# The first feed-forward product as 2x2 blocks, seven block products for eight, in three of four quarters

## The chip, the core and the metric

The kernel runs on one core of a Trainium2 chip. Measured is the device time of one call in microseconds. TensorE (PE) multiplies a stationary 128x128 weight with moving columns; VectorE (DVE), ScalarE (ACT) and GpSimd (POOL) do the elementwise work; SyncE (SP) issues the DMAs from DRAM. PEld is the weight load of TensorE.

## The reference

One step of a two-layer backbone over 640 tokens (128 of context, 512 latents) with 1024 features. A layer has a mixing part (three groups of heads and an output projection) and a feed-forward part of width 4096. The change concerns the second:

```python
h = rmsnorm(x, p['norm2_g']) * (1.0 + scale2) + shift2
x = x + gate2 * (relu(h @ W1) ** 2 @ W2)      # W1: 1024 x 4096, W2: 4096 x 1024
```

Shift, scale and gate (the modulation) come from a condition through a linear layer of each layer's own, with one column for the context's tokens and one for the latents'.

## The kernel before

Features lie on partitions, tokens along the free axis: x is eight tiles of 128 x 640. A product in float32 is made of three TensorE passes on float32r parts: high part of the weights by high part of the input, high by low, low by high. So each weight of 128 x 128 brings 3 x 2 matmuls of 320 columns, since a PSUM bank takes half of the tokens.

`feed_forward` (L1759) goes through the 4096 hidden features in four quarters. A quarter first makes eight units of the first product (f1): a unit is one block of 128 outputs, 8 blocks of input features x 3 passes x 2 halves = 48 matmuls (`fm`, L312 to 318). The input is not the normed one but x times its scale (zh, zl), with the two shifts as two extra columns, so the first half is 322 columns wide; `Norm.out` multiplies the product by 1/rms (un, L552), ACT adds the shift and takes the relu, DVE squares it (u, L1777) and `evac_split` (L306, L307) takes it apart into uh (a cast, ACT) and ul (a subtraction, DVE). Then come eight units of the second product (f2), again 48 matmuls each, that are added to x with the gate by three DVE instructions (`residual`, L565). A unit's PSUM tile (PA) is one of two, so unit m + 2 begins when DVE has emptied that of unit m.

Weights come through `Weights` (L282): a unit is two halves of 128 x 512 (256 KB), each fetched into wr by SP, cast to wh by ACT (L296) and subtracted to wl by DVE (L297).

The modulation of layer 1 is computed beside the feed-forward part of layer 0, as "fill" (`ada_rows`, L452 on): 112 pieces of weight of 256 KB (wa), each multiplied by one condition on POOL (junk, L481, summed by ACT, L482) and by the other on DVE (junk, L484). A fill step is two pieces: two POOL and two DVE products. There are 57 steps; f1 of the first quarter takes one per unit, f1 of the others one per two units, f2 one per unit, and what is left comes behind the last unit.

A scheduler orders the instructions when the program is built, each engine's list is fixed from then on, and an engine works through its list in order. Queues of interest: DVE's (weight splits, residuals, fill), POOL's (fill, the norm's sums of squares, the norm's power r, L257) and SP's (weights, fill, x).

In the last quarter `scaled` and `square` prepare the next layer's norm (zh, zl, L520; nsq, L512). The first product of layer 1 needs r for its first un.

## Time and profile before

| | |
|---|---|
| time, median of 3 runs | 1908.3 us (1906.05 to 1914.73) |
| span of the profiled execution | 1908.2 us |
| instructions | 31581 |
| PE busy | 1778.2 us (93%), 11796 matmuls |
| DVE busy | 1268.1 us (66%) |
| ACT busy | 863.5 us (45%) |
| POOL busy | 599.4 us (31%) |
| mean granted TensorE clock | 0.944 of full speed |

The span runs from the first to the last instruction of one execution. A share of busy time is an average over stages: the feed-forward part of layer 0 ends at 1005.4 us, that of layer 1 with the program.

### The profile page before, as it was taken

Reading aid. Unit: us, or ns where it says so; the run is one execution under the profiler, and the core shown is the slowest. Engines: PE = TensorE matmul, PEld = TensorE weight load, DVE = VectorE, ACT = ScalarE, POOL = GpSimd, SP = SyncE. Lnnn points to the kernel's source line nnn. Section 1 sums busy time; section 2 is a strip of 40 time slices with the busy share of each in tenths; the row PEclk is TensorE's granted clock in tenths of the full one; section 3 lists DMA queues with packets and bytes.
Section 4 is the critical chain, followed back from the end, with each engine's and each line's share of the span. In section 5 each row is a group of like instructions: output and inputs, shape, how many; then the busy total and the mean of one; then the engine's idle time right before and its main releaser. Section 6 shows DMA issues by size and latency. Waiting matters only on the chain. (4 is left out here: it accounts for less than half of the span.)

```text
span 1908.2 us, 31581 instructions
## 1 busy us (share of the span) xinstructions
PE 1778.2 (93%) x11796; PEld 1677.8 (88%) x11796; DVE 1268.1 (66%) x2427; ACT 863.5 (45%) x1921; POOL 599.4 (31%) x650
## 2 busy tenths in 40 slices
PE   6899975989999999999997899889998999999999
PEld 4798864889898998999996888768998999999999
DVE  7785778877879567584688766778657435344352
ACT  5553355765555253452555443376544324132230
POOL 4353345442546124150276455354203000000000
PEclk8998986999899999999997999889999999999999
...
GB/s 295 44 84 38 50 61 87 72 124 136 86 130 162 123 116 145 99 144 117 106 180 92 72 67 32 45 49 71 100 30 62 73 77 73 78 73 73 77 79 82
DMA packets 102329, 176.75 MB, mean 93 GB/s; under 512 B 11808, under 2 KB 27040, under 8 KB 102176
## 3 DMA queue, kind: packets, MB, share of 16 engines
...
q10 hardware_dynamic: 560, 0.18, 0.0%
...
## 5 line engine op out<-in xcount | busy, mean ns | idle before, releaser
L296 ACT CAST wh<-wr 128x512 fp32r<-128x512 f32 (+2 forms) x364 | 225.9, 622 | 560.7 <-PE fm L318 461.4
L297 DVE TENSOR_TENSOR wl<-wr,wh 128x512 fp32r<-128x512 f32 (+1 forms) x340 | 270.8, 802 | 116.7 <-issue 69.4
L481 POOL TENSOR_TENSOR junk<-wa,crow 128x512 f32<-128x512 f32 x112 | 175.2, 1583 | 288.4 <-DVE u L1777 194.5
L318 PE MATMUL fm<-zh,wh 128*128 128x322 f32 (+1 forms) x1088 | 252.2, 315 | 13.8 <-ACT zh L519 8.2
L318 PE MATMUL fm<-zl,wh 128*128 128x322 f32 (+1 forms) x1088 | 253.5, 314 | 2.2 <-DVE zl L520 1.4
L318 PE MATMUL fm<-zh,wl 128*128 128x322 f32 (+1 forms) x1088 | 252.2, 313 | 0.0
L318 PE MATMUL fm<-uh,wh 128*128 128x320 f32 x1024 | 235.8, 312 | 13.1 <-DVE x L565 13.1
L318 PE MATMUL fm<-ul,wh 128*128 128x320 f32 x1024 | 237.2, 311 | 0.1
L318 PE MATMUL fm<-uh,wl 128*128 128x320 f32 x1024 | 234.9, 311 | 0.0
L318 PEld LDWEIGHTS fm<-zh,wh 128*128 128x128 f32 x1088 | 185.6, 192 | 15.1 <-ACT zh L519 8.4
L318 PEld LDWEIGHTS fm<-zl,wh 128*128 128x128 f32 x1088 | 185.9, 192 | 4.0 <-DVE zl L520 2.1
L318 PEld LDWEIGHTS fm<-zh,wl 128*128 128x128 f32 x1088 | 185.9, 192 | 0.2 <-issue 0.2
L318 PEld LDWEIGHTS fm<-uh,wh 128*128 128x128 f32 x1024 | 173.1, 190 | 14.1 <-issue 14.0
L318 PEld LDWEIGHTS fm<-ul,wh 128*128 128x128 f32 x1024 | 173.6, 190 | 0.8 <-DVE ul L307 0.8
L318 PEld LDWEIGHTS fm<-uh,wl 128*128 128x128 f32 x1024 | 173.0, 190 | 0.0
L565 DVE SCALAR_TENSOR_TENSOR x<-fm,mod,x 128x128 f32<-128x128 f32 (+2 forms) x192 | 72.5, 432 | 134.4 <-PE fm L318 134.4
L552 DVE TENSOR_TENSOR un<-fm,nR 128x640 f32<-128x640 f32 x68 | 55.8, 823 | 108.7 <-PE fm L318 108.7
L784 PE MATMUL tm<-wl,hhi 128*128 128x256 f32 (+2 forms) x400 | 120.5, 302 | 4.9 <-POOL wl L297 4.9
L783 PE MATMUL tm<-wh,hhi 128*128 128x256 f32 (+2 forms) x400 | 120.5, 302 | 0.3 <-ACT xpad L628 0.2
L785 PE MATMUL tm<-wh,hlo 128*128 128x256 f32 (+2 forms) x400 | 120.0, 300 | 0.0
L484 DVE SCALAR_TENSOR_TENSOR junk<-wa,crow 128x512 f32<-128x512 f32 x112 | 115.2, 1067 | 0.0
L784 PEld LDWEIGHTS tm<-wl,hhi 128*128 128x128 f32 x400 | 81.2, 203 | 5.8 <-POOL wl L297 5.2
...
## 6 DMA issues: line engine op xcount, KB each, us to landing
...
wa<-in_w_adaT SPq DMA_DIRECT2D x112, 256.0 KB, 3.2
...
xsave<-x SPq DMA_DIRECT2D x24, 320.0 KB, 2.2
x<-xsave SPq DMA_DIRECT2D x24, 320.0 KB, 4.2
x<-in_xT SPq DMA_DIRECT2D x16, 320.0 KB, 5.6
out_yT<-x SPq DMA_DIRECT2D x8, 320.0 KB, 2.2
```

What stands on the lines that cost most here:

```text
L296: act.copy(out=hi[:, :w], in_=raw[:, :w])
L297: (pool if n in ON_POOL else vec).tensor_tensor(out=lo[:, :w], in0=raw[:, :w], in1=f(hi[:, :w]), op=ALU.subtract)
L318: pe.matmul(o, w, xx[k][:, ts], start=s, stop=e)
L481: pool.tensor_tensor(out=junk, in0=raws[i], in1=row[v][h], op=ALU.mult)
L484: vec.scalar_tensor_tensor(out=junk, in0=raws[i], scalar=1.0, in1=row[v][h], op0=ALU.mult, op1=ALU.mult, accum_out=sum_)
L552: vec.tensor_tensor(out=v2(t_), in0=fl[:, 2:1022].rearrange("p (h t) -> p h t", h=2)[:, :, :HT], in1=v2(self.R), op=ALU.mult)
L565: vec.scalar_tensor_tensor(out=x[m][:, t0:t0 + n], in0=src, scalar=mods[l][:, j, m, v:v + 1], in1=x[m][:, t0:t0 + n], op0=ALU.mult, op1=AL ...
L783: pe.matmul(ps[:, i, :n], hh[k][:, ts], hi[:, c:c + n], start=s, stop=False)
L784: pe.matmul(ps[:, i, :n], hh[k][:, ts], lo[:, c:c + n], start=False, stop=False)
L785: pe.matmul(ps[:, i, :n], hl[k][:, ts], hi[:, c:c + n], start=False, stop=e)
```

## The change

The first product of quarters 1 to 3 is made in pairs of units (m and m + 4). The block matrix of two output blocks by two halves of the input features, times two halves of features by two halves of tokens, takes eight block products; the Winograd form of Strassen's scheme takes seven (L1911 on, `pair`): four with sums of weight blocks (S1 to S4, made by POOL, L1791) or sums of input blocks (T1 to T4), and three with plain blocks. A block product is 4 k x 3 passes = 12 matmuls of 320 columns, a pair 84. Three PSUM banks (ffx, ffz, ffy) hold the sums; ACT copies a bank to SBUF between blocks, DVE adds the next bank to it (L1937, L1943, L1945). The square of the relu becomes one DVE instruction (u, L1893), and uh and ul follow as before.

The first quarter stays as it was. During units 0 to 3 of its second product `expanded` makes the normed input, which no longer has extra columns, and the sums T1 to T4 in 28 tiles that live to the end of the layer: per k four pieces on DVE, four on ACT, four POOL subtractions of 128 x 320 (L1869), and the two parts of each. To make room for them x goes to DRAM (xsave) after each unit of every second product and comes back one unit ahead in the next quarter.

Weights come through `Stream` (in place of `Weights` for this part): up to seven halves fetched and two split ahead. A pair's seven weight blocks are split as before (ACT L1804, DVE L1805). Buffers: 48 long tiles for 44, 13 of passage (Y) for 10, 7 raw weights for 4, 5 low parts for 4; the rotary tables moved into long tiles. With 7 raw buffers three more halves are fetched at the program's start. The fill is paced anew: one step per unit in the first quarter's f1, none in pairs, none in units 0 to 3 of the first quarter's f2, two in every other unit of f2.

```diff
-NG, NX, NXS = 44, 6, 10
-NWR, NWH, NWL = 4, 6, 4
+NG, NX, NXS = 48, 6, 13
+NWR, NWH, NWL = 7, 6, 5
...
+    FETCHED, AHEADS = 7, 2
...
+        def pair(self, n1, n2):                       # class Stream
...
+                for key, x0, x1, op in (("S1", "21", "22", ALU.add), ("S2", "S1", "11", ALU.subtract),
+                                        ("S3", "11", "21", ALU.subtract), ("S4", "12", "S2", ALU.subtract)):
+                    box[key] = Y([P, 512], name="wS")
+                    pool.tensor_tensor(out=box[key], in0=box[x0], in1=box[x1], op=op)
...
+            self.src += [(1, lambda key=key: take(key)) for key in ("11", "12", "S2", "S1", "S3", "S4", "22")]
...
+        for k in range(4):                            # expanded
+            h1, h2 = normed(k), normed(k + 4)
...
+            for o, i0, i1 in ((h_(ta, 0), h_(h1, 1), h_(h1, 0)), (h_(ta, 1), h_(h2, 1), h_(ta, 0)),
+                              (h_(tb, 0), h_(h2, 1), h_(h1, 1)), (h_(tb, 1), h_(h2, 0), h_(ta, 1))):
+                pool.tensor_tensor(out=o, in0=i0, in1=i1, op=ALU.subtract)
...
+            go(px, "B11", True)                       # pair
+            act.copy(out=v1[:, 0], in_=px)
+            go(pz, "B21", True)
+            vec.tensor_tensor(out=v1[:, 0], in0=v1[:, 0], in1=pz, op=ALU.add)
+            go(px, "T2", False)
+            act.copy(out=v1[:, 1], in_=px)
+            go(py, "T1", True)
+            act.copy(out=sy, in_=py)
+            go(px, "T3", False)
+            vec.tensor_tensor(out=v2_[:, 1], in0=sy, in1=px, op=ALU.add)
+            go(py, "B22", False)
+            vec.tensor_tensor(out=v1[:, 1], in0=v1[:, 1], in1=py, op=ALU.add)
+            go(px, "T4", False)
+            act.copy(out=v2_[:, 0], in_=px)
...
+                if q and m + 1 < KD:
+                    load_x(xsave, m + 1)
+                if q == 0 and m < 4:
+                    next(expand)
...
+                nc.sync.dma_start(a["yT"][:, m] if l == DEPTH - 1 and q == 3 else xsave[:, m], x[m])
...
+                for _ in range(0 if q == 0 and m < 4 else 2):
                     fill.step()
```

How the lists change, at three places. First, VectorE at the start of the second product of layer 0's second quarter, from behind the residual of unit 0 to that of unit 1 (x is the residual, junk the fill, wl a weight split). Before:

```order
L297 TENSOR_TENSOR wl_8051<-wr_8048,wh_8050 128x512
L297 TENSOR_TENSOR wl_8081<-wr_8078,wh_8080 128x512
L484 SCALAR_TENSOR_TENSOR junk_8283,adares_8272<-wa_8201,crow_6011 128x512
L484 SCALAR_TENSOR_TENSOR junk_8351,adares_8272<-wa_8278,crow_6008 128x512
L491 TENSOR_TENSOR adapt_8203<-adares_7316 128x16
L484 SCALAR_TENSOR_TENSOR junk_8361,adares_8272<-wa_8285,crow_6011 128x512
L565 SCALAR_TENSOR_TENSOR x_5061<-fm_7969,mod_86,x_5061 128x128
L565 SCALAR_TENSOR_TENSOR x_5061<-fm_7969,mod_86,x_5061 128x192
L565 SCALAR_TENSOR_TENSOR x_5061<-fm_7969,mod_86,x_5061 128x320
```
After:

```order
L1805 TENSOR_TENSOR wl_8211<-wr_8113,wh_8210 128x512
L484 SCALAR_TENSOR_TENSOR junk_8171,adares_8051<-wa_8159,crow_6026 128x512
L484 SCALAR_TENSOR_TENSOR junk_8242,adares_8051<-wa_8166,crow_6023 128x512
L484 SCALAR_TENSOR_TENSOR junk_8252,adares_8051<-wa_8173,crow_6026 128x512
L484 SCALAR_TENSOR_TENSOR junk_8256,adares_8051<-wa_8247,crow_6023 128x512
L1805 TENSOR_TENSOR wl_8276<-wr_8178,wh_8275 128x512
L484 SCALAR_TENSOR_TENSOR junk_8266,adares_8051<-wa_8254,crow_6026 128x512
L484 SCALAR_TENSOR_TENSOR junk_8337,adares_8051<-wa_8261,crow_6023 128x512
L565 SCALAR_TENSOR_TENSOR x_7984<-fm_8082,mod_86,x_7984 128x128
L565 SCALAR_TENSOR_TENSOR x_7984<-fm_8082,mod_86,x_7984 128x192
L565 SCALAR_TENSOR_TENSOR x_7984<-fm_8082,mod_86,x_7984 128x320
```
Six fill products stand between the two residuals, where three stood; seven stand ahead of the first of them, and the next units have seven and five. GpSimd's list at that place, before (fill alone, spread over f1 and f2):

```order
L481 TENSOR_TENSOR junk_8191<-wa_8116,crow_6010 128x512
L481 TENSOR_TENSOR junk_8196<-wa_8123,crow_6009 128x512
L481 TENSOR_TENSOR junk_8275<-wa_8194,crow_6010 128x512
L481 TENSOR_TENSOR junk_8280<-wa_8201,crow_6009 128x512
L481 TENSOR_TENSOR junk_8353<-wa_8278,crow_6010 128x512
```
After, the last weight sums of the pairs (wS) and the start of the fill:

```order
L1791 TENSOR_TENSOR wS_7704<-wr_7698,wr_7700 128x512
L1791 TENSOR_TENSOR wS_7706<-wS_7704,wr_7696 128x512
L1791 TENSOR_TENSOR wS_7708<-wr_7696,wr_7698 128x512
L1791 TENSOR_TENSOR wS_7710<-wr_7702,wS_7706 128x512
L481 TENSOR_TENSOR junk_8054<-wa_7371,crow_6025 128x512
L481 TENSOR_TENSOR junk_8059<-wa_7378,crow_6024 128x512
L481 TENSOR_TENSOR junk_8068<-wa_8057,crow_6025 128x512
L481 TENSOR_TENSOR junk_8073<-wa_8064,crow_6024 128x512
```
The fill that follows is 26 products in a row; the next weight sums stand behind them.

Second, VectorE in the first product of layer 1. Before, one unit:

```order
L552 TENSOR_TENSOR un_18812<-fm_18751,nR_16175 128x640
L297 TENSOR_TENSOR wl_18903<-wr_18900,wh_18902 128x512
L1777 TENSOR_TENSOR u_3937_18819<-relu_18816 128x640
L297 TENSOR_TENSOR wl_18933<-wr_18930,wh_18932 128x512
L307 TENSOR_TENSOR ul_18822<-u_3937_18819,uh_18821 128x640
```
After, the larger part of one pair (v is what ACT copied out of PSUM, ffx, ffy and ffz are the banks):

```order
L1937 TENSOR_TENSOR v_3884_17590<-v_3884_17590,ffz_17588 128x320
L1805 TENSOR_TENSOR wl_17678<-wr_17450,wh_17677 128x512
L1805 TENSOR_TENSOR wl_17695<-wr_17593,wh_17694 128x512
L1805 TENSOR_TENSOR wl_17712<-wr_17599,wh_17711 128x512
L1943 TENSOR_TENSOR v_3885_17591<-sy_17592,ffx_17587 128x320
L1805 TENSOR_TENSOR wl_17763<-wS_17603,wh_17762 128x512
L1945 TENSOR_TENSOR v_3884_17590<-v_3884_17590,ffy_17589 128x320
L1805 TENSOR_TENSOR wl_17780<-wS_17601,wh_17779 128x512
L1893 SCALAR_TENSOR_TENSOR u_3909_17728<-v_3884_17590 128x640
L1805 TENSOR_TENSOR wl_17797<-wS_17605,wh_17796 128x512
L1893 SCALAR_TENSOR_TENSOR u_3912_17734<-v_3885_17591 128x640
L307 TENSOR_TENSOR ul_17731<-u_3909_17728,uh_17730 128x640
```
A pair (two units) has seven splits, three additions from PSUM and four instructions of 640, where two units had four splits and six of 640; no fill stands here in either.

Third, VectorE behind the last unit of layer 0, to the norm's v, on which r and the first un of layer 1 rest. Before:

```order
L520 SCALAR_TENSOR_TENSOR zl_11145<-x_5379,amul_89,zh_11144 128x512
L720 TENSOR_REDUCE ls_11607<-lp_11606 128x2
L484 SCALAR_TENSOR_TENSOR junk_11169,adares_10890<-wa_11160,crow_6008 128x512
L484 SCALAR_TENSOR_TENSOR junk_11179,adares_10890<-wa_11167,crow_6011 128x512
L484 SCALAR_TENSOR_TENSOR junk_11183,adares_10890<-wa_11174,crow_6008 128x512
L722 TENSOR_TENSOR nlam_11609<-le_11608 128x1
L484 SCALAR_TENSOR_TENSOR junk_11193,adares_10890<-wa_11181,crow_6011 128x512
L723 TENSOR_SCALAR nlam_11609<-nlam_11609 128x1
L484 SCALAR_TENSOR_TENSOR junk_11197,adares_10890<-wa_11188,crow_6008 128x512
L484 SCALAR_TENSOR_TENSOR junk_11207,adares_10890<-wa_11195,crow_6011 128x512
L484 SCALAR_TENSOR_TENSOR junk_11211,adares_10890<-wa_11202,crow_6008 128x512
L535 TENSOR_SCALAR v_2427_11310<-nss_11304 128x5
```
After:

```order
L520 SCALAR_TENSOR_TENSOR zl_11462<-x_11328,amul_89,zh_11461 128x128
L520 SCALAR_TENSOR_TENSOR zl_11462<-x_11328,amul_89,zh_11461 128x512
L720 TENSOR_REDUCE ls_11855<-lp_11854 128x2
L722 TENSOR_TENSOR nlam_11857<-le_11856 128x1
L723 TENSOR_SCALAR nlam_11857<-nlam_11857 128x1
L535 TENSOR_SCALAR v_2580_11558<-nss_11552 128x5
```
The nine products between zl and v are gone from there; all fill stands ahead of the last residual.

## Rows read from the trace of the kernel before

**Rows 1.** Page, busy time of the engines; DMA rate in the 40 slices.
```profile
PE 1778.2 (93%) x11796; PEld 1677.8 (88%) x11796; DVE 1268.1 (66%) x2427; ACT 863.5 (45%) x1921; POOL 599.4 (31%) x650
...
GB/s 295 44 84 38 50 61 87 72 124 136 86 130 162 123 116 145 99 144 117 106 180 92 72 67 32 45 49 71 100 30 62 73 77 73 78 73 73 77 79 82
```

**Rows 2.** Busy us per engine, TensorE clock, DMA share, GB/s: quarters, then the layers' border.
```profile
652.10:771.80 119.70, 115.40 (x770) 114.92 (x770) 79.53 (x131) 49.76 (x114) 36.84 (x24) 0.99 0.40 124
...
1005.40:1035.40 30.00, 17.19 (x112) 16.63 (x110) 24.06 (x41) 14.92 (x37) 24.71 (x19) 0.78 0.34 104
1449.70:1563.20 113.50, 112.98 (x770) 112.72 (x769) 51.01 (x83) 34.79 (x66) 2.79 (x2) 1.00 0.26 75
1563.20:1676.70 113.50, 113.50 (x770) 113.50 (x769) 49.40 (x80) 34.25 (x65) 0.00 (x0) 1.00 0.26 75
```

**Rows 3.** VectorE in time, a first-product unit of layer 1: start, us, operation.
```profile
1584.63 0.82 DVE L552 TENSOR_TENSOR un<-fm,nR 128x640 f32<-128x640 f32 x1 [1.77 <-PE fm L318]
1585.37 0.68 DVE L297 TENSOR_TENSOR wl<-wr,wh 128x512 fp32r<-128x512 f32 x1
...
1589.21 0.83 DVE L307 TENSOR_TENSOR ul<-u,uh 128x640 fp32r<-128x640 f32 x1 [0.29 <-ACT uh L306]
1591.79 0.82 DVE L552 TENSOR_TENSOR un<-fm,nR 128x640 f32<-128x640 f32 x1 [1.75 <-PE fm L318]
```

**Rows 4.** VectorE, residuals of two neighbouring second-product units, layer 1.
```profile
1641.55 1.14 DVE L565 SCALAR_TENSOR_TENSOR x<-fm,mod,x 128x128 f32<-128x128 f32 x3 [2.77 <-PE fm L318]
...
1648.58 1.13 DVE L565 SCALAR_TENSOR_TENSOR x<-fm,mod,x 128x128 f32<-128x128 f32 x3 [2.77 <-PE fm L318]
```

**Rows 5.** TensorE in time, output projection of layer 1, single matmuls.
```profile
1400.22 0.31 PE L318 MATMUL wo<-mixh,wl 128*128 128x320 f32 x1
1400.37 0.30 PE L318 MATMUL wo<-mixh,wh 128*128 128x320 f32 x1
```

**Rows 6.** VectorE in time, second quarter of layer 0, first alone, then beside POOL.
```profile
712.62 0.69 DVE L484 SCALAR_TENSOR_TENSOR junk<-wa,crow 128x512 f32<-128x512 f32 x1
...
713.23 1.81 DVE L484 SCALAR_TENSOR_TENSOR junk<-wa,crow 128x512 f32<-128x512 f32 x1
...
714.97 1.77 DVE L297 TENSOR_TENSOR wl<-wr,wh 128x512 fp32r<-128x512 f32 x1
716.67 1.92 DVE L307 TENSOR_TENSOR ul<-u,uh 128x640 fp32r<-128x640 f32 x1
...
726.49 1.13 DVE L565 SCALAR_TENSOR_TENSOR x<-fm,mod,x 128x128 f32<-128x128 f32 x3
```

**Rows 7.** GpSimd in time, the same stretch.
```profile
700.61 1.30 POOL L481 TENSOR_TENSOR junk<-wa,crow 128x512 f32<-128x512 f32 x1 [1.36 <-DVE ul L307]
...
720.99 8.40 POOL L481 TENSOR_TENSOR junk<-wa,crow 128x512 f32<-128x512 f32 x5 [0.64 <-DVE junk L484]
```

**Rows 8.** Waits of TensorE: us in total, times, longest.
```profile
PE fm L318 <- DVE x L565: 15.8, 5, 4.5
...
PE nrb L544 <- POOL r L257: 9.2, 2, 8.8
...
PE fm L318 <- ACT bsh L557: 7.1, 4, 4.1
```

**Rows 9.** Groups by line and form: count, busy us, mean ns, idle before.
```profile
L318 PEld LDWEIGHTS fm<-uh,wh 128*128 128x128 f32 x1024 | 173.1, 190 | 14.1 <-issue 14.0
...
L437 POOL TENSOR_TENSOR wc<-wc,adat 128x256 f32<-128x256 f32 x48 | 40.5, 845 | 70.8 <-ACT adat L436 21.5 <-DVE wc L433 20.5 <-DMA wr<-in_W 13.3
...
L565 DVE SCALAR_TENSOR_TENSOR x<-fm,mod,x 128x320 f32<-128x320 f32 x64 | 34.6, 541 | 0.0
```

**Rows 10.** Start of layer 1's mixing: POOL's r, and VectorE's first un.
```profile
1027.63 1.18 POOL L257 TENSOR_TENSOR r<-v,mhalf 128x5 f32<-128x5 f32 x1
...
1034.38 1.55 DVE L552 TENSOR_TENSOR un<-fm,nR 128x640 f32<-128x640 f32 x2
```

**Rows 11.** DMA issues of the page: count, KB each, us to landing.
```profile
x<-xsave SPq DMA_DIRECT2D x24, 320.0 KB, 4.2
```

More of the change, by code (lines that the diff above doesn't have):

```diff
@@ L734, in mixing, with tables @@
         ropec, ropes = rope[:, 0], rope[:, 1]
-        def tables(gname, off, tag):
-            tcg = S([P, NT, 32], tag + "c", 1)
-            tsg = S([P, NT, 32], tag + "s", 1)
+        tabs2 = [G([P, 2, 2, NT, 32], name="tabs") for _ in range(2)]
+        def tables(gname, off, i):
+            tcg, tsg = (tabs2[i // 2][:, i % 2, j] for j in range(2))
             g = R(gname, off, 32)
@@ new lines, in build, with block @@
+    done = []
+    def block(out, w, xh, xl, first, last, on=False):
+        hi, lo = w
+        with after(done):
+            for i in range(4):
+                wh, wl = hi[:, i * P:(i + 1) * P], lo[:, i * P:(i + 1) * P]
+                for w_, x_, s_, e_ in ((wh, xh[i], first and i == 0, False), (wh, xl[i], False, False),
+                                       (wl, xh[i], False, last and i == 3)):
+                    for o, ts in out:
+                        mm = pe.matmul(o, w_, x_[:, ts], start=s_, stop=e_, skip_group_check=on)
+        done[:] = [mm]
@@ L1759, in feed_forward @@
     def feed_forward(l, nrm, fill):
-        names = []
+        W = Stream(l)
         for q in range(4):
-            names += [f"f1_{q}_{m}" for m in range(8)] + [f"f2_{q}_{m}" for m in range(8)]
-        W = Weights(l, names, AHEAD)
-        nxt = Norm()
+            if q == 0:
+                for m in range(8):
+                    W.unit(f"f1_{q}_{m}", 2)
+            else:
+                for m in range(4):
+                    W.pair(f"f1_{q}_{m}", f"f1_{q}_{m + 4}")
+            for m in range(8):
+                W.unit(f"f2_{q}_{m}", 2)
@@ new lines, in feed_forward, with hidden, squared @@
+        ex = {n: ([], []) for n in ("B11", "B21", "B22", "T1", "T2", "T3", "T4")}
+        expand = expanded(l, nrm, ex)
+        nxt = Norm()
+        full = slice(0, HT)
+        def hidden(v, m, uh, ul):
+            u = X([P, T], name="u2")
+            vec.scalar_tensor_tensor(out=u, in0=v, scalar=0.0, in1=v, op0=ALU.max, op1=ALU.mult)
+            uh[m], ul[m] = G([P, T], F32R, name="uh"), G([P, T], F32R, name="ul")
+            evac_split(uh[m], ul[m], u)
+        def squared(m, ps, uh, ul):
+            t_, b = nrm.out(ps)
+            act.activation(out=t_[:, :NCTX], in_=t_[:, :NCTX], func=AF.Identity, bias=b[:, 0:1])
+            act.activation(out=t_[:, NCTX:], in_=t_[:, NCTX:], func=AF.Identity, bias=b[:, 1:2])
+            hidden(t_, m, uh, ul)
@@ new lines, in early @@
+        def early(uh, ul):
+            ps = [PA("fm") for _ in range(2)]
+            ws = [[W.next() for _ in range(2)] for _ in range(2)]
+            for k in range(KD):
+                with after(nrm.last):
+                    if k == 4:
+                        nrm.rows()
+                    if k == 5:
+                        nrm.spread()
+                for w, p_ in zip(ws, ps):
+                    hi, lo = w[k // 4]
+                    fm(zhalves(p_), hi[:, (k % 4) * P:], lo[:, (k % 4) * P:], nrm.zh, nrm.zl, [k], 0, KD - 1)
+            for m, p_ in enumerate(ps):
+                squared(m, p_, uh, ul)
@@ new lines, in plain, with pair, go @@
+        def plain(m, uh, ul):
+            ps = PA("fm")
+            for h in range(2):
+                block(zhalves(ps), W.next(), nrm.zh[4 * h:4 * h + 4], nrm.zl[4 * h:4 * h + 4], h == 0, h == 1)
+            squared(m, ps, uh, ul)
+        def pair(ms, uh, ul):
+            px, pz, py = PA("ffx")[:, 0, :HT], PB("ffz")[:, :HT], PB("ffy")[:, :HT]
+            v1, v2_ = X([P, 2, HT], name="v1"), X([P, 2, HT], name="v2")
+            sy = Y([P, HT], name="sy")
+            def go(out, n, first):
+                block([(out, full)], W.next(), *ex[n], first, True, not first)
+            go(px, "B11", True)
[12 more added lines that the diff above has]
+            act.copy(out=v2_[:, 0], in_=px)
+            for v, m in zip((v1, v2_), ms):
+                hidden(v.rearrange("p h t -> p (h t)"), m, uh, ul)
@@ L1765, in feed_forward @@
         mark(f"{l}ff")
-        ready = first_units(W, names[:2], nrm)
         for q in range(4):
-            uh, ul = [], []
+            uh, ul = [None] * 8, [None] * 8
+            if q == 0:
+                early(uh, ul)
+                for m in range(8):
+                    mark(f"{l}ff")
+                    if m >= 2:
+                        plain(m, uh, ul)
+                    fill.step()
+            else:
+                for m in range(4):
+                    mark(f"{l}ff")
+                    pair((m, m + 4), uh, ul)
+                load_x(xsave, 0)
@@ L1788, in feed_forward @@
+                ps = PA("fm")
+                for h in range(2):
+                    block(halves(ps), W.next(), uh[4 * h:4 * h + 4], ul[4 * h:4 * h + 4], h == 0, h == 1)
                 residual(l, 5, m, ps)
+                nc.sync.dma_start(a["yT"][:, m] if l == DEPTH - 1 and q == 3 else xsave[:, m], x[m])
                 if q == 3:
-                    nc.sync.dma_start(a["yT"][:, m] if l == DEPTH - 1 else xsave[:, m], x[m])
                     if l + 1 < DEPTH:
```

95 lines of the change are left out of this document (70 added, 25 removed).

## Prediction

> **What bounds the kernel now.** I read first the busy shares of the page [rows 1], then the busy times by stretch over the feed-forward parts [rows 2], then what ends the waits there. TensorE (PE) is busy 93% of the span at nearly full clock. In the quarters of layer 1 it is busy 112.98 to 113.50 of 113.50 us at a granted clock of 1.00 while VectorE (DVE) does 49 to 51 us and GpSimd (POOL) next to nothing: that stage is bound by the number of matmuls alone. In layer 0 a quarter takes 119.7 us, with DVE at 79.5 us and POOL at 37, since the modulation of layer 1 (the fill) is computed there; PE is idle for 119.7 - 115.4 = 4.3 us of it, a wait for a residual [rows 2, 8]. So there are two regimes: layer 1 pays for every matmul taken away, layer 0 pays only as far as DVE and POOL have room.
>
> A unit of the first product repeats every 7.16 us (from one un to the next, 1584.63 to 1591.79 [rows 3]), one of the second every 7.03 us (1641.55 to 1648.58 [rows 4]); 7.03 / 48 = 0.1465 us per matmul of 320 columns.
>
> The DVE prices depend on POOL. Alone, a 128x512 DVE instruction with two SBUF inputs takes 0.68 us (one every 0.61 us) and a 640 one 0.83 us (every 0.75). While POOL works they take 1.77 to 1.92 us [rows 6], and POOL's 512 product goes from 1.30 us to 8.40 / 5 = 1.68 us [rows 7]. With both queues full one DVE instruction passes per POOL instruction, every 1.70 us: each POOL instruction adds 1.70 - 0.61 = **1.09 us** to DVE. That is the most the rows show. The least, over a loose stretch, comes from [rows 2]: a layer-0 quarter has 79.53 us of DVE, a layer-1 quarter 49.40; of the 30.1 more, 24 products at 0.61 are 14.6 and some 0.6 small ones, so 14.9 us go with 24 POOL instructions, **0.62** each. I use 0.62 to 1.09, near the upper end where both queues are full. Instructions that read PSUM are not touched: the residual takes 1.13 us in either case [rows 4, 6].
>
> **The change part by part.**
>
> *Matmuls.* A pair takes 84 matmuls for 96: 2 x 7.16 - 84 x 0.1465 (12.31) = 2.01 us. 24 pairs: -48.2 us, 24.1 in each layer. A pair's weights change at every matmul instead of every second one. The loads are counted once per matmul already, and where the output projection runs single 320-column matmuls on fresh weights they follow each other at 0.15 us [rows 5]; I add nothing.
>
> *DVE and POOL in a pair.* DVE: 7 weight splits x 0.61, 3 PSUM additions x 0.54 (the 128x320 residual row [rows 9]), 4 instructions of 640 x 0.75 = 8.9 us. POOL: 4 weight sums, where it had nothing in layer 1; they add 4 x 0.62 to 1.09 = 2.5 to 4.4. Together 11.4 to 13.3 us against PE's 12.31. DVE so becomes about as long as PE. ACT has 7 casts, 4 copies and 2 halves of the split, some 7.4 us by its own rows, and stays hidden. Inside a pair the block T4 writes on the bank that DVE must have read after T3; PE has one block (12 x 0.1465 = 1.76 us) to cover that, enough for a lone split plus the addition (0.68 + 0.54), not for a held-up one (1.77 + 0.54, 0.5 over). Bounds: 0 and 1.5 us per pair (1.0 DVE excess, 0.5 the wait). The middle of 11.4 to 13.3 is PE's own time, so DVE alone costs nothing there and the wait at T4 falls due about every second time; I take 0.3: +3.5 per layer.
>
> A rule of the Trainium skill bears here (page "SBUF — State Buffer", section "Who interferes with whom"): a DVE instruction with two SBUF inputs contends with a GpSimd one that reads SBUF, and whoever starts first holds the shared port pair for the whole instruction while the other fully blocks. The trace agrees on which instructions suffer; on how much, it shows less than a whole POOL instruction, 1.09 us for 1.30. By the whole instruction a pair's DVE would be 14.1 us; that is the third rival.
>
> *Expansion, second product of the first quarter.* In units 0 to 3 DVE gets, per unit, four norm pieces and four splits (4.3 us by the pitches above) on top of two weight splits and the residual (2.3): 6.6 us. POOL adds four subtractions of 320 (256 columns took 0.845 us [rows 9]), so 4 x some 0.8 us: about 9.8 against 7.03. Four units overrun by 11 us; one unit's slack of the two PSUM buffers (some 6 us) covers part: +5.3 in layer 1 (3 to 9). In layer 0 DVE comes to that place late already (its first-quarter stall, the longest of the five, is 4.5 us [rows 8]), so the overrun is paid whole: +11 (8 to 17).
>
> *Fill moved.* Pairs carry no fill; the 16 steps of a quarter (32 POOL and 32 DVE products) now all fall into eight f2 units, where before 8 of 12 did. In the second and third quarter POOL has 26 products in a row, and DVE 25 before the residual of unit 3 (7, 6, 7, 5). DVE alone: 25 x 0.61 + 8 splits x 0.61 + 1.5 + four residuals of 1.1 = 26.0 us. POOL adds 26 x 0.62 to 1.09 = 16 to 28. So the residual of unit 3 ends 42 to 54 us into f2; PE needs it after five units, 35.2 us. Overrun 7 to 19. Both queues are full here, so the upper end is the nearer one; some products start before f2, and I take 15, less the 4.3 of before: **+10.7 in each of the two quarters** (+3 to +15). The later units have few products, but PE, the bound there, cannot regain it. Check: DVE alone 73 us over such a quarter ((44 splits + 32 products) x 0.61 + 12 x 0.54 + 16 x 0.75 + 8 x 1.1) plus 48 POOL instructions x 0.62 to 1.09 gives 103 to 125 us, against 105.4 of matmuls. In the fourth quarter the last products and the next layer's norm share units 1 to 4, near 10 us each for 7.03; after the buffer's slack +7 (5 to 9).
>
> *Start of layer 1.* Before, POOL's r is queued behind leftover fill: it runs at 1027.63 and the first un at 1034.38 [rows 10], 29 us after the last residual at 1005.4 [rows 2]; PE waits 8.8 us for r and 4.1 for the shift [rows 8]. After, no fill is left; v follows the last zl directly. I count 15 to 17 us from residual to un: **-12** (-6 to -14: the two named waits are 12.9).
>
> *Rest.* The residual parked in DRAM adds loads of 4.2 us [rows 11], issued one unit (7.03 us) ahead, so hidden unless SP's queue is held by a fill load that waits for its buffer; stores don't hold PE. More buffers mean three extra 256 KB loads at the start, ahead of the second modulation's: 0.79 MB at the first slice's 295 GB/s [rows 1] is 0 to 2.7 us, I take +1. The mixing parts keep their orders but for small exchanges: 0 (-3 to +3).
>
> **Sum.** Layer 1: -24.1 + 5.3 + 3.5 = -15.3. Layer 0: -24.1 + 11 + 21.4 + 7 + 3.5 - 12 = +6.8. Start +1. Together -7.5 on the profiled span of 1908.2 us, which is the median of the runs (1908.3) to 0.1: **1901 us**.
>
> **The rivals.**
>
> *A, collisions are cheap.* The stalls above sum to 51.7 us. If a POOL instruction costs DVE half of what I took, because their gaps fit into each other, half goes: 1901 - 26 = **1875**. For it: un, residuals and PSUM additions leave POOL free time at DVE. Against it: in the full stretch DVE instruction after instruction took 1.77 us or more [rows 6].
>
> *B, pairs run at DVE's pace: slower than before.* If the S sums cost DVE the full 1.09 and T4 waits each time, a pair loses 1.5 us instead of 0.3: 24 x 1.2 = 29, **1930**. It decides from 0.85 us per POOL sum on, where 8.9 + 4 x 0.85 passes PE's 12.31; to end slower than before it takes 0.6 us per pair, twice what I took. For it: both queues are dense in a pair; against it: POOL has only 4 x 1.3 to 1.7 us of work in 12.3.
>
> *The whole lock* (the rule named above): a sum costs 1.30, a pair 1.5 us more than I took (+36), and each fill quarter's overrun grows to 25 (+20): **1957**. No row shows over 1.09.
>
> *No saving, weight loads bound.* A load is recorded at 0.190 us [rows 9]; were it not hidden behind a single 320-column matmul, 2016 x (0.190 - 0.1465) = +88 us, **1989**. The pace of [rows 5] speaks against it.
>
> **How the numbers follow.** My sum (1890 to 1914) 0.52, A 0.26, B 0.17, the whole lock 0.03, no saving 0.02. A and B spread by some 10 us about their middles; the range goes 5 us past either middle, 1870 to 1935, and leaves out 0.08 below and 0.10 above. A measurement here can tell about 0.5% (9.5 us): faster means below 1898.8. Of my sum's cases 0.18 lie below that, 0.33 within, 0.01 above; with A, faster is 0.44; same 0.33; B and the two last make slower 0.23.
>
> **What would show it.** Right: first products at 12.3 to 12.7 us per pair in layer 1; its weight splits at 1.7 us where POOL runs; PE waiting for the DVE residual in f2 units 2 to 5 of layer 0's second and third quarter, some 15 us each; those quarters still near 120 us, layer 1's near 107; first un of layer 1 some 15 us after the last residual. Wrong: layer 0's quarters near 108 (A), pairs of 13.5 us or more with PE waiting for the additions in both layers (B), or matmuls of 0.19 us pace. What I may have missed: x loads that land late behind fill loads, and a clock that falls after the longer stalls (0.78 was granted between the layers).

## The result and the profile after

The changed kernel takes 1900.1 us (median of 11 runs, 1893.61 to 1906.51) where the kernel before takes 1909.8 in the same series. The ratio is 0.9942 with a 95% interval of 0.9928 to 0.9957: 0.6% faster, and clear of no change. The predicted 1901 us and its direction hold. The profiled execution's span is 1896.4 us, 11.8 less than that of before; the sums below are made on the two profiled executions.

The page of the kernel after, busy times, to be laid beside [rows 1]:

```profile
PE 1735.2 (92%) x11508; PEld 1628.9 (86%) x11508; DVE 1432.1 (76%) x2587; ACT 915.3 (48%) x2009; POOL 797.5 (42%) x778
```

PE has 43 us less, DVE 164 us more, POOL 198 us more. TensorE's longest wait in total, the one for residuals, has grown from 15.8 us to 42.5 ([rows 8] for before; us in total, times, longest):

```profile
PE fm L1834 <- DVE x L565: 42.5, 17, 6.9
```

The stages by the trace, each from its first matmul to the first of the next one, in us. The last column is what the prediction's sum had for the stage.

| stage | before | after | difference | forecast |
|---|---|---|---|---|
| start and mixing of layer 0 | 518.9 | 513.4 | -5.4 | +1 |
| layer 0, first quarter, f1 | 68.9 | 65.1 | -3.8 | 0 |
| layer 0, first quarter, f2 (expansion) | 64.1 | 74.9 | +10.8 | +11 |
| layer 0, f1 of quarters 1, 2, 3 (pairs) | 57.0, 57.0, 57.0 | 52.9, 49.5, 49.7 | -19.0 | -20.6 |
| layer 0, f2 of quarters 1 and 2 | 62.6, 62.7 | 76.4, 75.6 | +26.6 | +21.4 |
| layer 0, f2 of quarter 3 | 56.2 | 62.9 | +6.6 | +7 |
| border of the layers | 30.9 | 21.1 | -9.8 | -12 |
| layer 1, mixing and first f1 | 471.3 | 473.5 | +2.3 | 0 |
| layer 1, first quarter, f2 (expansion) | 56.3 | 60.0 | +3.7 | +5.3 |
| layer 1, f1 of quarters 1, 2, 3 (pairs) | 57.3 each | 49.3, 49.3, 49.1 | -24.2 | -20.6 |
| layer 1, f2 of quarters 1, 2, 3 | 56.3 each | 56.4, 56.5, 56.2 | +0.5 | 0 |

Busy time by stretch, after (columns as in [rows 2]): f2 of layer 0's first quarter; pairs and f2 of its second; f2 of its last; then of layer 1 the expansion's f2, four pairs and their f2.

```profile
578.60:653.50 74.90, 59.73 (x386) 58.31 (x385) 74.60 (x106) 40.19 (x86) 58.05 (x37) 0.95 0.38 120
653.50:706.40 52.90, 49.85 (x337) 49.33 (x338) 46.96 (x65) 26.32 (x51) 23.24 (x14) 1.00 0.35 109
706.40:782.70 76.30, 61.43 (x385) 59.47 (x385) 71.51 (x107) 33.18 (x85) 61.94 (x38) 0.96 0.66 223
957.40:1020.30 62.90, 58.61 (x386) 57.89 (x385) 56.88 (x89) 33.21 (x73) 42.16 (x34) 0.97 0.62 202
1514.90:1574.90 60.00, 58.05 (x386) 57.79 (x385) 48.78 (x72) 28.59 (x53) 34.60 (x26) 0.97 0.35 109
1574.90:1624.20 49.30, 49.30 (x339) 49.12 (x337) 38.89 (x56) 26.00 (x49) 10.21 (x7) 1.00 0.29 87
1624.20:1680.60 56.40, 56.40 (x387) 56.40 (x386) 24.36 (x41) 11.70 (x20) 15.61 (x11) 1.00 0.52 167
```

Pairs and f2 together, the second quarter of layer 0 is 129.2 us long and the third 125.0 where each was 119.7; a quarter of layer 1 is 105.7 where it was 113.5. In layer 1 the pairs run at PE's pace: four in 49.30 us, 12.32 each, with the clock at 1.00. In layer 0 the gain of the pairs comes back in f2: DVE is busy 71.5 of 76.3 us, POOL 62, and PE only 61.4.

VectorE's own rows show why (f2 of layer 0's second quarter, from the residual of unit 0 to that of unit 1; start and duration in us):

```profile
722.01 1.12 DVE L565 SCALAR_TENSOR_TENSOR x<-fm,mod,x 128x128 f32<-128x128 f32 x3
723.05 0.71 DVE L1805 TENSOR_TENSOR wl<-wr,wh 128x512 fp32r<-128x512 f32 x1
723.68 1.80 DVE L484 SCALAR_TENSOR_TENSOR junk<-wa,crow 128x512 f32<-128x512 f32 x1
...
725.42 0.68 DVE L484 SCALAR_TENSOR_TENSOR junk<-wa,crow 128x512 f32<-128x512 f32 x1
...
726.03 0.68 DVE L484 SCALAR_TENSOR_TENSOR junk<-wa,crow 128x512 f32<-128x512 f32 x1
...
726.65 1.76 DVE L484 SCALAR_TENSOR_TENSOR junk<-wa,crow 128x512 f32<-128x512 f32 x1
...
728.34 1.76 DVE L1805 TENSOR_TENSOR wl<-wr,wh 128x512 fp32r<-128x512 f32 x1
730.03 1.76 DVE L484 SCALAR_TENSOR_TENSOR junk<-wa,crow 128x512 f32<-128x512 f32 x1
...
731.72 0.68 DVE L484 SCALAR_TENSOR_TENSOR junk<-wa,crow 128x512 f32<-128x512 f32 x1
...
732.34 1.12 DVE L565 SCALAR_TENSOR_TENSOR x<-fm,mod,x 128x128 f32<-128x128 f32 x3
```

Of the six fill products and two splits between the two residuals, four take 1.76 to 1.80 us and the others 0.68 to 0.71; the residual, which reads PSUM, takes 1.12. From residual to residual 10.3 us pass (722.01 to 732.34), where PE needs 7.03 for a unit. TensorE then waits, and what follows the wait is slow:

```profile
733.61 0.87 PE L1834 MATMUL fm<-uh,wh 128*128 128x320 f32 x2 [3.02 <-DVE x L565]
734.28 0.73 PE L1834 MATMUL fm<-ul,wh 128*128 128x320 f32 x2
734.81 0.73 PE L1834 MATMUL fm<-uh,wl 128*128 128x320 f32 x2
...
736.95 0.47 PE L1834 MATMUL fm<-uh,wh 128*128 128x320 f32 x2
737.26 0.45 PE L1834 MATMUL fm<-ul,wh 128*128 128x320 f32 x2
```

After the stall of 3.02 us two matmuls take 0.53 us (734.28 to 734.81) until 736.9, then 0.29 to 0.31. The granted clock by stretch, first the wait, then the next 4 us, then the rest:

```profile
730.60:733.60 3.00, 0.00 (x0) 0.03 (x1) 3.00 (x8) 0.98 (x4) 2.36 (x3) 0.99 0.74 209
733.60:737.60 4.00, 3.99 (x17) 4.00 (x18) 4.00 (x6) 1.97 (x6) 3.28 (x2) 0.58 0.92 300
737.60:742.40 4.80, 4.80 (x33) 4.55 (x31) 4.80 (x8) 2.25 (x7) 3.61 (x3) 1.00 0.56 190
```

0.58 of full speed is mostly the lower of the clock's two levels, 1.2 GHz: the 3 us of waiting cost another 0.42 x 4.0 = 1.7 us behind them. Of the three waits of 3 us and more in this f2, two are followed by such a stretch. PE is idle for 76.3 - 61.4 = 14.9 us of it: 13.5 in six waits for residuals, the last of them ahead of the next pair, and 1.4 in two for ul. It is busy 5.0 us longer than the 56.4 of an undisturbed f2. Two slow stretches, which cost 1.7 us each, make 3.4 of that; the rest may be the starting up after eight waits, which is not shown singly.

At the border of the layers, before's rows are [rows 10]. After (VectorE, then POOL; the last residual, v, the first un; r):

```profile
1020.50 1.14 DVE L565 SCALAR_TENSOR_TENSOR x<-fm,mod,x 128x128 f32<-128x128 f32 x3 [2.25 <-PE fm L1834]
...
1029.38 0.17 DVE L535 TENSOR_SCALAR v<-nss 128x5 f32<-128x5 f32 x1 [4.45 <-PE nss L533]
1035.45 4.99 DVE L669 SCALAR_TENSOR_TENSOR nt<-x,amul,nR 128x128 f32<-128x128 f32 x6 [5.90 <-ACT nR L545]
1040.36 0.81 DVE L552 TENSOR_TENSOR un<-fm,nR 128x640 f32<-128x640 f32 x1
```

```profile
1029.70 1.18 POOL L257 TENSOR_TENSOR r<-v,mhalf 128x5 f32<-128x5 f32 x1
```

No fill stands between. Counted from the start of the last residual, r runs after 9 us and the first un after 20, where before it was 22 and 29.

### The profile page after: what moved, and what is told of

Same layout as the page of the kernel before. It is cut to its first block, busy times and chain, and to the rows that moved or that the text cites. A ratio compares the mean times of both kernels' runs of the same rounds, so it can differ in the third digit from the quotient of the medians.

```text
span 1896.4 us, 31841 instructions
## 1 busy us (share of the span) xinstructions
PE 1735.2 (92%) x11508; PEld 1628.9 (86%) x11508; DVE 1432.1 (76%) x2587; ACT 915.3 (48%) x2009; POOL 797.5 (42%) x778
## 5 line engine op out<-in xcount | busy, mean ns | idle before, releaser
L1834 PE MATMUL fm<-uh,wh 128*128 128x320 f32 x1024 | 239.2, 315 | 42.5 <-DVE x L565 42.5
L1804 ACT CAST wh<-wr 128x512 fp32r<-128x512 f32 x232 | 143.0, 617 | 221.2 <-PE fm L1834 134.0
L1805 DVE TENSOR_TENSOR wl<-wr,wh 128x512 fp32r<-128x512 f32 x232 | 204.0, 890 | 55.7 <-issue 38.9
L1791 POOL TENSOR_TENSOR wS<-wr,wr 128x512 f32<-128x512 f32 x48 | 76.4, 1591 | 168.3 <-DMA wr<-in_W 145.7
L484 DVE SCALAR_TENSOR_TENSOR junk<-wa,crow 128x512 f32<-128x512 f32 x112 | 139.1, 1271 | 9.0 <-DMA wa<-in_w_adaT 9.0
L565 DVE SCALAR_TENSOR_TENSOR x<-fm,mod,x 128x128 f32<-128x128 f32 (+2 forms) x192 | 72.3, 430 | 79.3 <-PE fm L1834 79.3
L482 ACT ACTIVATE junk<-junk 128x512 f32<-128x512 f32 x112 | 70.3, 628 | 89.2 <-POOL junk L481 89.2
L1804 ACT CAST wh<-wS 128x512 fp32r<-128x512 f32 x96 | 59.4, 621 | 108.0 <-PE fm L1834 37.3
L296 ACT CAST wh<-wr 128x512 fp32r<-128x512 f32 (+2 forms) x108 | 66.3, 624 | 72.8 <-PE fm L318 41.5
L1834 PE MATMUL ffx<-eh,wh 128*128 128x320 f32 x288 | 89.5, 311 | 3.1 <-ACT v L1935 3.0
L1834 PE MATMUL ffx<-eh,wl 128*128 128x320 f32 x288 | 88.8, 308 | 0.0
L1834 PE MATMUL ffx<-el,wh 128*128 128x320 f32 x288 | 88.8, 308 | 0.0
```

What stands on the lines that cost most here:

```text
L482: act.activation(out=junk, in_=junk, func=AF.Copy, accum_out=sum_)
L484: vec.scalar_tensor_tensor(out=junk, in0=raws[i], scalar=1.0, in1=row[v][h], op0=ALU.mult, op1=ALU.mult, accum_out=sum_)
L565: vec.scalar_tensor_tensor(out=x[m][:, t0:t0 + n], in0=src, scalar=mods[l][:, j, m, v:v + 1], in1=x[m][:, t0:t0 + n], op0=ALU.mult, op1=AL ...
L1791: pool.tensor_tensor(out=box[key], in0=box[x0], in1=box[x1], op=op)
L1804: act.copy(out=hi, in_=raw)
L1805: vec.tensor_tensor(out=lo, in0=raw, in1=f(hi), op=ALU.subtract)
```

## The experiments

Every ratio is to the kernel before in the same series, with its 95% interval. The stage times are from the profiled execution of each.

**The buffers alone.** On the kernel before:

```diff
-NG, NX, NXS = 44, 6, 10
-NWR, NWH, NWL = 4, 6, 4
+NG, NX, NXS = 48, 6, 13
+NWR, NWH, NWL = 7, 6, 5
... (rotary tables in two long tiles, DMA scratch of 1024)
```

> The kernel before with only the changed kernel's buffers (48 long tiles, 13 Y, 7 raw weights, 5 low parts, rotary tables in long tiles, the smaller DMA scratch); fill, units and x as before. Theory 1: the 5.4 us that layer 0's mixing part lost and the 3.8 us of its first f1 units come from the buffers, so this runs about 9 us faster than before, some 1900 us, and its feed-forward quarters stay at 113.5 and 119.7 us. Rival: those microseconds come from the new order of the feed-forward part or are chance; then it lies within 3 us of the kernel before.

Measured: 1911.7 us, ratio 1.0012 (0.9998 to 1.0027): no gain in the whole time. Its profiled execution is the fastest of its twelve. In it the mixing part of layer 0 took 449.9 us, as short as in the changed kernel (450.6; 456.2 before), and the first f1 2.0 us less than before, while layer 0 from its first f2 to its end took 3.7 us more (420.4 for 416.7). A single profile says little of 5 us, however. Two other kernels here (all fill on DVE, without and with the expansion's subtractions there) have, by their traces, the same list of instructions on every engine up to the feed-forward part, and took 454.1 and 449.0 us for it. The difference goes with the granted clock; the same stretch in the one, and in the other (columns as in [rows 2]):

```profile
411.20:440.00 28.80, 24.97 (x164) 24.08 (x164) 26.34 (x52) 21.09 (x52) 15.51 (x14) 0.76 0.53 169
440.00:472.00 32.00, 30.06 (x228) 29.14 (x227) 19.60 (x43) 17.02 (x44) 5.97 (x7) 0.89 0.32 106
```

```profile
411.10:438.40 27.30, 22.58 (x166) 21.86 (x166) 26.24 (x52) 21.10 (x53) 15.58 (x14) 0.87 0.57 184
438.40:467.30 28.90, 26.96 (x227) 26.05 (x225) 19.32 (x43) 16.83 (x44) 5.96 (x7) 1.00 0.35 114
```

0.76 and 0.89 in one execution, 0.87 and 1.00 in the other: 4.6 us for the same work.

All the profiles together say more. The eleven kernels with the new buffers have the same lists in this part, but for a record or two, and took 449.0 to 454.4 us for it. The three with the old ones (before, the fill moved, the fill on DVE in the kernel before) have another order and took 456.2 to 458.1. The two groups do not overlap. So the 5.4 us between the profiles of before and after go with the buffers and the order that the scheduler makes for them, as far as one profile of each kernel tells; what in them does it was not tried. The medians of the two differ by 9.7 us, the profiles by 11.8.

**The fill's new pace alone.** On the kernel before:

```diff
-    FF1 = (1, 0, 1, 0, 1, 0, 1, 0)
+    FF1 = (0, 0, 0, 0, 0, 0, 0, 0)
...
-                if m in FF2:
+                for _ in range(0 if q == 0 and m < 4 else 2):
                     fill.step()
```

> The kernel before with only the fill paced as in the changed one: none in the first product of quarters 1 to 3, none in f2 units 0 to 3 of the first quarter, two steps in every other f2 unit. Theory 1: the fill in f2 is what stalls layer 0, whatever the first product is: f2 of quarters 1 and 2 takes 73 to 77 us (62.6 before), of quarter 3 some 63 (56.2), the first quarter's f2 loses its 4.5 us stall, the border of the layers loses some 10 us; together 1908 + 27 + 6 - 4 - 10 = about 1925 us. Rival: in the changed kernel it is the weight sums and the x loads that crowd f2, and the fill alone fits; then f2 stays near 63 us and the time falls to some 1898.

Measured: 1928.6 us, ratio 1.0097 (1.0073 to 1.0121). f2 of quarters 1, 2 and 3 takes 72.1, 72.2 and 63.9 us, the border 21.1. f2 of the second quarter:

```profile
708.40:780.50 72.10, 62.00 (x386) 60.85 (x385) 67.53 (x109) 32.73 (x86) 49.57 (x31) 0.93 0.56 176
```

So the pace by itself makes f2 9.5 us longer in two quarters and 7.6 in the third, without a pair in the kernel, and the rival is out; the border gives 9.8 back. The first quarter's f2 kept its length (64.0), against the expectation. The changed kernel's f2 is 4 us longer still. The pairs bring that, since with plain units and all else kept (the next experiment) it is 71.8 us: PE waits 13.5 us for residuals there and 9.1 here, and the last two of those waits, 2.7 us, come at its end, behind weight sums for the next pairs on POOL and 4.6 us in which DVE waits for a piece of wa.

**Plain units with all the rest kept.** On the changed kernel:

```diff
-            if q == 0:
+            if True:
                 for m in range(8):
                     W.unit(f"f1_{q}_{m}", 2)
...
-                for m in range(4):
-                    pair((m, m + 4), uh, ul)
+                for m in range(8):
+                    plain(m, uh, ul)
...
-                if q == 0 and m < 4:
-                    next(expand)
```

> The changed kernel with plain units in quarters 1 to 3 as well, and without the expansion; buffers, fill pace and x in DRAM stay. Theory 1: pairs bring their full 8.0 us per quarter in both layers, less the expansion (10.8 in layer 0, 3.7 in layer 1): 1900 + 48 - 14.5 = about 1934 us. Rival: in layer 0 DVE and POOL set the time over a whole quarter, so that what f1 gains f2 gives back; then layer 0 is no longer than with pairs, and the time is some 1920 us.

Measured: 1923.4 us, ratio 1.0060 (1.0042 to 1.0078). So the pairs with their expansion are worth 23 us, not 34, and the rival (1920 us) is the nearer. By the two profiles they give 24.4 us in layer 1, less 3.7 for the expansion, and 20.5 in layer 0's f1, of which 10.1 go to the expansion and 6.4 are lost again in f2. f2 of the second quarter takes 71.8 us here (72.1 with x kept in SBUF, above), so the residual in DRAM costs nothing there.

**POOL's half of the fill left out**, then **DVE's half left out**, on the changed kernel. Each leaves out one half of the products of layer 1's modulation.

```diff
                 if 2 * h + v in ROWS_POOL:
-                    pool.tensor_tensor(out=junk, in0=raws[i], in1=row[v][h], op=ALU.mult)
-                    act.activation(out=junk, in_=junk, func=AF.Copy, accum_out=sum_)
+                    pass
```

```diff
                 else:
-                    vec.scalar_tensor_tensor(out=junk, in0=raws[i], scalar=1.0, in1=row[v][h], op0=ALU.mult, op1=ALU.mult,
-                                             accum_out=sum_)
+                    pass
```

> The changed kernel without POOL's half of the fill (its products and ACT's sums are left out, so layer 1 has a wrong modulation for one of the two conditions); DVE's half, with its queue of seven, six, seven and five products ahead of the residuals, stays. Theory 1: the stall is the collision on DVE with POOL, since DVE alone needs 26 us to the residual of unit 3 where PE needs it at 35: f2 of layer 0's quarters 1 to 3 comes down to 56 to 58 us, quarter 0's f2 by 2 to 4, together some 35 to 40 us, to about 1862. Rival: it is the length of DVE's queue, or x arriving late from DRAM: then f2 stays above 70 us and the time above 1890.

> The changed kernel without DVE's half of the fill (left out, so layer 1 has a wrong modulation for one condition); POOL's 112 products stay. Theory 1: the stall needs both halves, DVE's queue and POOL's collisions with it: alone DVE has 11 us to the residual of unit 3, and 26 collisions at most 28 us more, 39 for 35; but it stands idle for part of them, so f2 falls to 57 to 62 us, the time to about 1865. Rival: POOL alone is enough, by holding each split and each u; then f2 stays above 68 us.

Measured: 1848.7 us (ratio 0.9678, 0.9657 to 0.9699) and 1848.2 us (0.9676, 0.9650 to 0.9701). f2 of quarters 1, 2, 3 is 58.3, 57.9, 56.5 us without POOL's half, 57.4, 57.1, 57.1 without DVE's. f2 of the second quarter in each:

```profile
695.00:753.30 58.30, 56.88 (x386) 56.62 (x385) 42.79 (x112) 11.78 (x21) 13.89 (x10) 1.00 0.84 297
```

```profile
694.60:752.00 57.40, 56.92 (x386) 56.66 (x385) 37.12 (x48) 32.64 (x85) 55.28 (x38) 1.00 0.87 307
```

Without POOL's products DVE does in 42.8 us what took it 71.5, with the same queue of its own. POOL has 28 instructions fewer in that stretch (31 products are gone, three more weight sums fall into it), so each had cost DVE 28.7 / 28 = 1.03 us. Without DVE's products POOL is still busy for 55.3 us, and PE is idle for 0.5. The stall needs both. x from DRAM is not late in either. Both gained more than expected (51 us for 35 to 40). Without POOL's half the three f2 came to about the length that was expected, and gave 42 us; the first quarter's f2 gave 7.0 where 2 to 4 were expected, and the pairs of layer 0 gave 4.3, which had not been counted.

**All fill on DVE**, and then the expansion's subtractions and the pairs' weight sums too, on the changed kernel:

```diff
-    ROWS_POOL = (1, 2)
+    ROWS_POOL = ()
```

> The changed kernel with both halves of the fill on DVE, nothing of it on POOL or ACT: DVE gets 112 more products, each 0.61 us alone. Theory 1 (a POOL product costs DVE 1.09 us where both queues are full, more than the product itself): a unit of f2 then holds 8 x 0.61 + 2 x 0.61 + 1.1 = 7.2 us of DVE for PE's 7.03, and f2 of layer 0's quarters 1 and 2 comes down from 76 to 57 to 62 us; together some 35 to 45 us, about 1860 us. Rival (DVE's queue is simply too long, and POOL takes work off it): f2 grows by half of the 18 us of added DVE work, and the time rises to about 1920 us.

Measured: 1865.6 us, ratio 0.9755 (0.9731 to 0.9779). f2 of quarters 1 and 2: 58.3 and 58.2 us.

```profile
706.40:764.70 58.30, 56.88 (x386) 56.61 (x386) 58.18 (x160) 11.79 (x21) 6.74 (x5) 1.00 0.85 287
```

DVE now makes all of the products in 58.2 busy us of an f2, where half of them beside POOL's took it 71.5. What is left has moved: the pairs behind those f2 take 53.7 and 54.3 us, where PE now waits for the addition L1943.

```diff
-                pool.tensor_tensor(out=o, in0=i0, in1=i1, op=ALU.subtract)
+                vec.tensor_tensor(out=o, in0=i0, in1=i1, op=ALU.subtract)
```

> As the one before, and the expansion's subtractions on DVE as well (sixteen of 128x320 in each layer). Theory 1: a subtraction costs DVE 0.4 us instead of up to 0.9 by collision: the first quarter's f2, 74.9 us in layer 0 and 60.0 in layer 1 in the changed kernel, falls to 60 to 64 and 57 to 59; 2 to 5 us under the kernel before it. Rival: DVE has no room in these units at all, and the added 1.6 us per unit come out at the end, up to 5 us more.

Measured: 1856.5 us, ratio 0.9708 (0.9685 to 0.9731), 9 us less than the kernel before it. The first quarter's f2 falls from 72.3 to 62.7 us in layer 0 and from 60.0 to 56.25 in layer 1, where the expansion is then free; the first four pairs of layer 0 give 8.6 back. These stages make 4.8 us; the two kernels whose mixing parts were compared above are these two, and 5.1 us of the difference of the profiles lie there (layer 1's mixing part with the first f1 takes 3.4 back).

```diff
-                    pool.tensor_tensor(out=box[key], in0=box[x0], in1=box[x1], op=op)
+                    vec.tensor_tensor(out=box[key], in0=box[x0], in1=box[x1], op=op)
```

> The changed kernel with fill, expansion and the pairs' weight sums all on DVE; POOL has nothing left of them. A quarter's sums are 16 x 0.61 = 9.8 us of DVE. Theory 1: where DVE has room (layer 1, 39 of 49.3 us busy in the pairs) nothing changes; in layer 0 a sum costs DVE about the same on either engine, so the time lies within 5 us of the kernel before it. Rival: in a pair DVE's added work comes in front of the PSUM additions that PE waits for, and a pair takes 13 us or more: 24 x 0.7 = 17 us longer.

Measured: 1846.3 us, ratio **0.9659** (0.9637 to 0.9681): 3.4% faster than the kernel before, the fastest complete version here. Layer 1's pairs do not change (49.2 us for four), those of layer 0 take 57.4, 52.3 and 51.7 us (60.3, 53.7 and 54.4 with the sums on POOL). That is 7 us, where at most 5 were expected: by these times a weight sum in layer 0 costs DVE more from POOL than as its own. The rest of the 10 lies in the mixing parts (3.6 us longer in layer 0; in layer 1, with the first f1, 8.3 shorter), and no run shows why. VectorE in f2 of its second quarter, residual to residual:

```profile
718.66 1.15 DVE L565 SCALAR_TENSOR_TENSOR x<-fm,mod,x 128x128 f32<-128x128 f32 x3
719.70 0.70 DVE L1805 TENSOR_TENSOR wl<-wr,wh 128x512 fp32r<-128x512 f32 x1
720.30 0.70 DVE L484 SCALAR_TENSOR_TENSOR junk<-wa,crow 128x512 f32<-128x512 f32 x1
...
724.57 0.71 DVE L484 SCALAR_TENSOR_TENSOR junk<-wa,crow 128x512 f32<-128x512 f32 x1
...
725.19 1.15 DVE L565 SCALAR_TENSOR_TENSOR x<-fm,mod,x 128x128 f32<-128x128 f32 x3
```

Nine instructions of 512 stand there in 5.5 us (719.70 to 725.19), one every 0.61: 6.5 us from residual to residual, within PE's 7.03.

**The same fill on DVE in the kernel before, and in the kernel with plain units.**

> The kernel before with both halves of the fill on DVE, nothing else changed. Theory 1: its stalls of 4.3 us in three quarters go, and behind the last unit POOL's r no longer waits behind fill, though DVE's leftover products do stay (twenty for ten): 10 to 20 us less, 1890 to 1900 us. Rival: DVE's queue gets longer and the stalls grow: 1910 us or more.

Measured: 1901.1 us, ratio 0.9943 (0.9923 to 0.9962). f2 of quarters 1 and 2 is 59.0 and 58.9 us, the border 26.1. The gain is at the lower edge of what was expected.

> The changed kernel with plain units in every quarter (no pairs, no expansion) and all fill on DVE: the partner without pairs of the kernel with all on DVE (1846 us). With the fill split between POOL and DVE the pairs were worth 23 us. Theory 1: without collisions they are worth more: 24 us in layer 1 and some 11 in layer 0 (pairs there took 161 us for 172), so this kernel runs at about 1882 us. Rival: their worth in layer 0 is limited by something else, and the difference stays about 23 us: 1870 us.

Measured: 1890.4 us, ratio 0.9911 (0.9896 to 0.9925), beside 0.9659 for its partner with pairs and everything on DVE: 48 us by the ratios, 44 by the medians (of two series). With the work shared between DVE and POOL the pairs were worth 23 (1923.4 to 1900.1). This is more than was expected (1882 us), but it is not the 48 us by count of matmuls. By the two profiles, 43.8 us apart, f1 gives 25.3 us in layer 1 and only 11.1 in layer 0, f2 gives 3 and the mixing parts, where there are no pairs, 4. In layer 0's pairs other work still comes between: four take 51.7 to 57.4 us there and 49.2 in layer 1.

**Less fill in layer 0.** One modulation of seven made in layer 1's first f1, eleven steps a quarter for sixteen; once with everything on DVE, once on the changed kernel as it is:

```diff
-        f1 = Part(ada_rows(ADA_T) if l == 0 else iter(()), 57)
+        f1 = Part(ada_rows([t for t in ADA_T if t != (1, 5)]), 49) if l == 0 else Part(ada_rows([(1, 5)]), 8)
...
-                for _ in range(0 if q == 0 and m < 4 else 2):
+                for _ in range(0 if q == 0 and m < 4 else 2 if q == 0 else (2, 1, 1, 2, 1, 1, 2, 1)[m]):
```

> The kernel with all on DVE, and one of the seven modulations (the gate of layer 1's feed-forward part, 8 of 57 steps) moved into layer 1's first quarter of f1, one step per unit; the f2 units of layer 0's quarters 1 to 3 take eleven steps for sixteen. Theory 1: in the kernel with all on DVE a layer-0 quarter needs some 103 us of DVE for 105.4 of PE, so its pairs still wait (51.7 to 57.4 us for 49.2, 12 in sum) and f2 has 2 us over; with 92 us of DVE most of it goes: 8 to 14 us less, about 1835 us; layer 1's f1 pays 0 to 3. Rival: what is left there are waits of order, not of amount, and stay: within 4 us of the kernel with all on DVE.

> The changed kernel with POOL's share of the work as it is, and only the same modulation moved into layer 1 and eleven steps for sixteen per quarter. Theory 1: per f2 unit 1.4 steps cost DVE 1.4 x 2 x (0.61 + 1.09) = 4.8 us, with splits and residual 7.1 for 7.03: f2 of layer 0's quarters 1 and 2 falls from 76 to 60 to 66 us, of quarter 3 from 62.9 to 58 to 60: some 25 to 30 us, about 1873 us. Rival: POOL's products come in one row whatever their number, and the first units stall as before: f2 falls only by the five steps at the end, under 6 us a quarter, about 1885 us.

Measured: 1859.7 us, ratio 0.9731 (0.9712 to 0.9749), so slower than with everything on DVE (0.9659); and 1896.7 us, 0.9927 (0.9911 to 0.9944), beside 0.9942 (0.9928 to 0.9957) for the changed kernel: no gain that is clear of noise. Both expectations fell. In the first, the pairs of quarters 2 and 3 did fall to 49.2 us, but the border grew from 21.2 to 26.9, the expansion's f2 in layer 1 from 56.3 to 61.8, and layer 1's mixing part with the first f1 from 468.5 to 474.4. In that f2 the last of the moved fill stands ahead of the expansion, and PE waits 3.7 us for ul. TensorE at that border waits for the last modulation:

```profile
977.45 0.54 PE L318 MATMUL fm<-zh,wh 128*128 128x322 f32 x2 [3.57 <-DVE adapt L491]
```

In the second, f2 of quarters 1 and 2 is 71.3 and 68.9 us (76.4 and 75.6 before): the rival's five steps less, not the fall to 60 to 66, since POOL's products still stand in a row; and border, mixing part with first f1, and f2 in layer 1 lose 13.8.

## Why the prediction was right, step by step

**The frame held.** Layer 1 is paid in matmuls, layer 0 in DVE and POOL. Fresh weights at every matmul cost nothing: 336 matmuls of four pairs in 49.3 us are 0.147 each. The rival without a saving is out. The total fits to 1 us, but that is luck: against the table's last column, stages that came out too long by 11.8 us and too short by 16.0 nearly cancel.

**The price of a collision** was the right cause and nearly the right size: 1.09 taken as the most, 1.03 measured as the difference of two runs. Rival A (half of the price) is out in layer 0.

**The whole lock.** The rule in the Trainium skill (page "SBUF — State Buffer", section "Who interferes with whom") names which instructions meet, and the runs agree: with all of that work on DVE its 512 instructions run at one every 0.61 us. A whole POOL instruction per meeting (1.29 us) is more than the 1.03 of the runs; 1957 us was not reached.

**f2 of layer 0's second and third quarter: right in idle time, short in the sum.** 15 us were forecast and 14.9 are idle, 13.5 of them for residuals (12.9 in the third quarter). The queue was right too: the residual of unit 3 ends 50.3 and 50.2 us into f2, where 42 to 54 were forecast. The step that failed is the one that took the overrun for the whole loss: PE's busy time behind the waits, 3.4 us of it by the slow clock, adds 5.0 us, of which before, with one wait, had 1.9 (62.64 - 4.3 - 56.4). So the difference is +13.7 and +12.9 for 10.7.

**Pairs in layer 1: too dear by 3.5 us.** The step put four weight sums into each pair. The trace shows POOL doing 7 in four pairs, the first of them begun just before, and 11 in the f2 before the next ones (the last two rows of busy time by stretch, above), so that only 5 are left for the next four pairs: `Stream` fetches seven halves ahead, and the sums run when their weights land. POOL there (start, us):

```profile
1589.68 1.74 POOL L1791 TENSOR_TENSOR wS<-wr,wr 128x512 f32<-128x512 f32 x1
1598.20 1.29 POOL L1791 TENSOR_TENSOR wS<-wr,wS 128x512 f32<-128x512 f32 x1 [6.78 <-DMA wr<-in_W]
1652.78 1.30 POOL L1791 TENSOR_TENSOR wS<-wr,wr 128x512 f32<-128x512 f32 x1 [53.29 <-DMA wr<-in_W]
```

It waits for wr, not for the pair. DVE is then busy 38.9 of 49.3 us, and neither DVE's amount nor the wait at T4 shows: rival B is out in layer 1. With all sums on DVE the pairs there stay at 49.2, so DVE has room for all 16.

**Pairs in layer 0** came 1.6 us under the forecast gain, with the first four 3.4 us behind the others: fill left over from the first quarter's f2 stands there before the residual of unit 7 and before ACT's copy, for which PE waits 2.3 us.

**Expansion** 10.8 for 11 and 3.7 for 5.3; in layer 1 it is wholly collision, as it is free (56.25 us) when DVE makes the subtractions. **Border** -9.8 for -12: 20 us from the last residual to the first un instead of 15 to 17. The next units' matmuls stand between on PE (v waits 4.45 us for nss), and six pieces of nt, 4.99 us, ahead of un on VectorE.

**Not foreseen:** -5.4 us before the feed-forward part begins. The three loads at the start, put at +1, cost 0.2; the mixing part, put at 0 (-3 to +3), is 5.6 us shorter, as in every kernel with the new buffers. And -3.8 in the first f1 of layer 0, of which it was said that it stays as it was: that stage is 65.1 to 65.2 us in every kernel with `Stream` and 65.6 to 68.9 in those without. Its units too get their weights from `Stream` and their square from one instruction; which of the two does it was not tried.
